# The moving weight tiles of two matmul stages, shifted by 15 distances in SBUF

## The chip, the cores and the metric

The kernel runs on one core of one Trainium2 chip. The metric is the device time in microseconds (us) of one execution; with several runs, their median. The engines are PE (TensorE, the matrix engine, whose weight loads are listed apart as PEld), DVE (VectorE), ACT (ScalarE), POOL (GpSimd) and SP (SyncE, which here only starts DMA transfers).

## The reference

One decoder layer on x of 512 tokens by 1024 channels, in float32, cut to what matters here:

```python
proj = x @ w_in                               # q, k, v, pool_in, gate logits
y_attn = moba_attention(q, k, v, rel_bias) @ w_branch_attn
y_pool = multiscale_pool(p, w_pool_group, pool_scale) @ w_branch_pool
mixed = gates[:, :, 0] * y_attn + gates[:, :, 1] * y_pool
h = layer_norm(ALPHA * x + mixed @ w_out, ln1_g, ln1_b)          # the output projection
a, u = split(h @ w_ffn_in)                                        # 1024 -> 2 x 2816
f = (gelu(causal_dwconv(a, conv_w, conv_b)) * u) @ w_ffn_out      # the FFN's output, 2816 -> 1024
out = layer_norm(ALPHA * h + f, ln2_g, ln2_b)
```

## The kernel before, in words

**Every float32 product is three matmuls.** A float32 tile is split in two tiles of type float32r: hi is a copy by ScalarE (line 75), lo is the rest by VectorE (line 76). `mm3` (lines 241 to 246) then issues hi x hi (line 242), hi x lo or lo x hi (245, 246), each a matmul with its own weight load of 128 x 128. Of each matmul one operand is *stationary* (128 columns, loaded into PE beforehand) and one is *moving* (256 or 512 columns that stream through).

**Which operand moves.** In most stages (input projection, gates, branches, FFN's input: forms p, g, br, fi, sa, sb, sc) the weights are stationary and the activations move. In two stages it is the other way round: in the output projection (`wo_mm`, form wo) and in the FFN's output (`fo_mm`, forms foa, fob, fod, foe, fo_cut) the activations (mx, sd) are stationary and the weights move, 512 columns at a time, fo_cut 256.

**Weights** come in tiles of 128 x 1024, in the order of the list `chunks`. `fetch` loads one by DMA, splits it into hi and lo, and puts these into a slot of a ring of five (`slot`, with `RING = 5`); up to three tiles are fetched ahead (`LEAD = 3`). The last three of the eight w_out tiles go to a pool of their own (`ext`). A slot is 1088 elements wide (`SLOT = D + 64`), which is 17 x 256 bytes, so all slots begin at the same place modulo 256 bytes (192 in the built program). The activations that face them begin there too, as do xT, hT and the rest. So the *distance* of a matmul, the place of its moving tile less that of its stationary tile, is 0 modulo 256 bytes, with one exception: tiles that `slot` is asked for with `near` lie `BESIDE = 2` elements, 8 bytes, further on. These are the stationary weight tiles of the first four FFN-input blocks (256-column matmuls) and of all "seven-product" tiles:

```python
o = BESIDE if near else 0
return tuple(wp.tile([P, SLOT], F32R, ...)[:, o:o + n] for q in ("hi", "lo"))
```

**Seven products.** Pairs of tiles of the input projection, gates and FFN's input, and the FFN's output as a whole, are computed by a scheme with seven products in place of eight on half-size blocks. For the pairs these are 256-column matmuls (forms sa, sb, sc: f is the FFN's input, 84 matmuls for each of 17 pairs). For the FFN's output the seven products (`PRODUCTS`: T3, B11, B21, T1, T2, B22, T4) come one after the other. Each takes six weight tiles (p, c), whose 11 half-tiles are the moving operands, against two blocks of 128 tokens: 11 x 2 x 3 = 66 matmuls. Of the last product one token block runs with 512 columns (33 matmuls, foe) and the other in two halves of 256 (66 matmuls, fo_cut). While a product runs, the next ones' operands are formed by ACT, DVE and by DMAs from POOL that add one weight block to another in place.

**Order.** The instructions are written in this order and recorded by a layer that may move them by a modelled time; no order was given by hand around the change, other than what `fetch` and `product` say.

Of the kernel before, what the change touches and what calls it, by code (L numbers as in the profile page):

```python
# [9 lines left out]
F32R = mybir.dt.float32r  # L10
# [4 lines left out]
P = 128  # L15
S = 512
D = 1024
# [15 lines left out]
RING = 5  # L33
SLOT = D + 64
BESIDE = 2
TMP = 7
PLAIN = (3, 2)
WARM = 6
RAW = 1
KH = NF // 2  # L40
# [11 lines left out]
def layer_kernel(ctx: ExitStack, tc: tile.TileContext, xT, x, w_v, w_c, rel_bias, invcnt, w_group,  # L52
# [18 lines left out]
    def split(hi, lo, src, copy=None):  # L71
        if copy:
            copy(hi, src)
        else:
            state["hi"] = nc.scalar.activation(hi, src, AF.Copy)  # L75
        state["lo"] = nc.vector.tensor_tensor(lo, src, hi.bitcast(F32), op=ALU.subtract)  # L76
        return state["lo"]
# [30 lines left out]
    WO0 = len(chunks)  # L108
    chunks += [w_out[k * P:(k + 1) * P, :] for k in range(KT)]
    FI0 = len(chunks)  # L110
# [6 lines left out]
    FO0 = len(chunks)  # L117
# [3 lines left out]

    def slot(i, n, near=False):
        o = BESIDE if near else 0
        return tuple(wp.tile([P, SLOT], F32R, tag=f"w{q}", name=f"w{q}{i}", bufs=RING)[:, o:o + n]
                     for q in ("hi", "lo"))

# [2 lines left out]
    def fetch(pool=None, early=None):  # L129
        i = state["next"]  # L130
        state["next"] = i + 1
        for q, ahead in AHEAD.items():
            while coming[q]:
                key = coming[q][0]
                n, f = key
                lead_ = EARLY.get((n, f, q), ahead)
                if not homes.get((n, q)) or at[n, f, q] > i + (lead_ if q != "A" or (n, f - 1) in pair_of else 0):
                    break
                with ExitStack() as held:
                    if (n, f, q) == ("i", 1, "X"):  # L140
                        held.enter_context(tc.issue_after(state["neg"].ins))
                    if (n, f, q) in (("i", 1, "D"), ("i", 2, "A"), ("i", 2, "X"), ("i", 2, "D")):
                        held.enter_context(tc.issue_after(state["plain"].ins))
                    if (n, f, q) == ("i", 2, "X"):
                        held.enter_context(tc.issue_after(state["sum"].ins))
                    fetch_raw(coming[q].pop(0), q)
        if isinstance(chunks[i], tuple):
            ready[i] = (fetch_fo if i >= FO0 else fetch_seven)(i, *chunks[i])
            return
        raw = wp.tile([P, D], F32, tag="wraw", name=f"wraw{i}", bufs=3)  # L150
        if pool is None:
            hi, lo = slot(i, D, FI0 <= i < FI0 + COVER)
        else:
            hi = pool.tile([P, D], F32R, name=f"whi{i}")
            lo = pool.tile([P, D], F32R, name=f"wlo{i}")
        parts = 2 if early else 1
        for c in range(parts):
            sl = slice(c * (D // parts), (c + 1) * (D // parts))
            (nc.scalar if early else nc.sync).dma_start(raw[:, sl], chunks[i][:, sl])
            split(hi[:, sl], lo[:, sl], raw[:, sl])  # L160
            if c == 0 and early:
                state["w0"] = raw[:, sl]
                early()
        ready[i] = (hi, lo)
# [10 lines left out]
    def fetch_raw(key, q):  # L175
        a, u = pair_of[key]
        r = raws[key, q] = homes[key[0], q](key[1])
        if q == "A":
            nc.sync.dma_start(r, a)
        elif q == "D":  # L180
            nc.sync.dma_start(r, u[:, S:])
        elif key in SUMMED:
            state["plain"] = nc.sync.dma_start(r[:, :S], u[:, :S])
        else:
            v = r.rearrange("p (a c) -> p a c", a=2)
            (pst, pn), (est, _) = u.ap
            state["plain"] = nc.sync.dma_start(
                v, bass.AP(tensor=u.tensor, offset=u.offset, ap=[[pst, pn], [0, 2], [est, S]]))
            state["acc"] = nc.gpsimd.dma_start(  # L189
                v, bass.AP(tensor=a.tensor, offset=a.offset, ap=[[pst, pn], [u.offset + S - a.offset, 2], [est, S]]),  # L190
                accum_op=ALU.add)

    def fetch_seven(i, key, q):
        n = S if q == "D" else D
        raw = raws[key, "A" if q == "Y" else q]
        if q == "X" and key in SUMMED:
            with tc.issue_after(state["Y"].ins):
                for c, o in ((slice(S, D), raws[key, "D"]), (slice(0, S), raws[key, "A"][:, :S])):
                    nc.vector.tensor_tensor(raw[:, c], raw[:, :S], o, op=ALU.add)
        if q == "Y":  # L200
            with ExitStack() as held:
                if key == ("f", COVER // 2):
                    held.enter_context(tc.issue_after(state["h"].ins))

                for c, o in ((slice(0, S), raws[key, "X"][:, S:]), (slice(S, D), raw[:, :S])):
                    nc.vector.tensor_tensor(raw[:, c], o, raw[:, c], op=ALU.add)
        hi, lo = slot(i, n, True)
        state[q] = split(hi, lo, raw)
        return hi, lo
# [7 lines left out]
    def fetch_fo(i, name, c):  # L217
        sl = piece(c)
        n = sl.stop - sl.start
        step = {"T3": "=B11", "B11": "+B12", "T1": "+B22", "T2": "+B21", "T4": None}  # L220
        if name in step:
            raw = tw[:, sl]
        else:
            raw = wp.tile([P, D], F32, tag="wraw", name=f"wraw{i}", bufs=3)[:, :n]
            nc.sync.dma_start(raw, half(name, sl))
        hi, lo = slot(i, n)
        split(hi, lo, raw)
        then = step.get(name)
        if then and then[0] == "+":
            nc.gpsimd.dma_start(raw, half(then[1:], sl), accum_op=ALU.add)  # L230
        elif then:
            nc.sync.dma_start(raw, half(then[1:], sl))
        return hi, lo

    def weights(i):
        while state["next"] <= min(i + LEAD, state["limit"]):
            fetch()
        return ready[i]
# [102 lines left out]
    for kt in range(KT):  # L341
        xk = xr[kt // 4][:, kt % 4, :]
        if kt == 0:
            load_x(kt, xk, slice(0, 256), nc.vector.tensor_copy)
            fetch(early=lambda: load_x(kt, xk, slice(256, 512), nc.vector.tensor_copy))
        else:
            load_x(kt, xk)
            if kt % 2 == 0:
                fetch()
# [102 lines left out]
    def pool_sum(j, b, sign=1.0, eng=None):  # L452
        eng = eng or nc.gpsimd
        w = POOL_WINDOWS[j]
        pt = pb.tile([P, PAD + S], F32, tag="tmp", name=f"pt{j}", bufs=TMP)
        nc.gpsimd.memset(pt[:, :PAD], 0.0)
        state["pt"] = nc.scalar.activation(pt[:, PAD:], b, AF.Copy, scale=sign)
        cur, sh = pt, 1
        while sh < w:
            nxt = pb.tile([P, PAD + S], F32, tag="tmp", name=f"pw{j}_{sh}", bufs=TMP)  # L460
            o = 2 * sh - 1
# [251 lines left out]
    def gate_done(f, ba, u):  # L713
        if f < KT - 1:
            for br, v, scale in ((0, ba, 1.0), (1, u, -1.0)):
                nc.scalar.activation(v, v, AF.Sigmoid, scale=scale)
                nc.vector.tensor_tensor(branch[f, br], branch[f, br], v, op=ALU.mult)
            merged(f, branch[f, 0], branch[f, 1])
        else:
            for br, v, scale in ((0, ba, 1.0), (1, u, -1.0)):  # L720
                gslot[8 * br + f] = unused.pop(0)
                nc.scalar.activation(gslot[8 * br + f], v, AF.Sigmoid, scale=scale)
# [6 lines left out]
    for f in range(GSEVEN, KT):  # L729
        if f == KT - 1:  # L730
# [3 lines left out]
              lambda ba, u, f=f: gate_done(f, ba, u), first_half if f == KT - 1 else None)  # L734
# [427 lines left out]
```

## Time and profile before

| what | us |
|---|---|
| timed runs, median of 3 | 627.9 |
| timed runs, lowest and highest | 627.87, 630.2 |
| profiled execution, span from first to last instruction | 625.9 |
| PE busy in the span | 616.0 (98%) |
| DVE, ACT, POOL busy | 505.2, 353.8, 119.0 |
| output projection, from its first matmul to its end | 245.19 to 290.49 |
| the FFN's output, from its first matmul to its last one's end | 512.19 to 617.28 |

How to read it: the profiled execution is one run of its own; its span lies 2.0 us under the median of the timed runs. "Busy" of PE counts matmuls from start to a modelled end, and they overlap; the time that one matmul takes of the stream is therefore read from start to start in a timeline, or as a stretch's length divided by its number of matmuls. A group by form gives the mean from start to modelled end, in ns, which differs from the step to the next start by a constant, so that differences between forms carry over.

### The profile page before, as it was taken

To read this page: it belongs to the slowest core of one execution; us is meant where nothing else is said; L and a number is where in the kernel's file an instruction comes from. 1 tells how busy PE (TensorE), PEld (TensorE's weight loads), DVE (VectorE), ACT (ScalarE), POOL (GpSimd) and SP (SyncE) were. 2 spreads that over 40 slices of the span, in tenths; PEclk is the share of its full clock that TensorE was granted. 3 is DMA by queue.
4 is the path that set the end of the run, shared out by engine and by line. 5 is a ranking of instruction groups with operands and counts; after the bars stand their busy time and mean duration, and the time that the engine had idled before them with its cause. 6 is when DMAs were issued, how large, how long until landed. Compare 5 with 4: busy or idle time off the path is not lost.

```text
span 625.9 us, 10417 instructions
## 1 busy us (share of the span) xinstructions
PE 616.0 (98%) x3988; PEld 552.9 (88%) x3988; DVE 505.2 (81%) x780; ACT 353.8 (57%) x536; POOL 119.0 (19%) x131
## 2 busy tenths in 40 slices
PE   8999999999999999999999999999999999999994
PEld 6899998777788998889999999999999888888884
DVE  6978787776494788399998988898988869798886
ACT  6646777655644567125566565566656346555442
POOL 0133134323132101110110101101100302123302
PEclk9999999999999999999999999999999999999998
DMA  9566647422548515816668687687745996899805
GB/s 321 163 193 187 177 121 223 134 78 78 169 111 211 149 60 177 293 43 225 146 167 208 184 201 185 176 201 201 187 97 161 325 254 127 221 192 207 195 1 134
DMA packets 40545, 107.70 MB, mean 172 GB/s; under 512 B 4384, under 2 KB 4648, under 8 KB 40240
## 3 DMA queue, kind: packets, MB, share of 16 engines
q1 hardware_dynamic: 27264, 71.90, 34.8%
q0 software_dynamic: 12656, 34.10, 28.0%
q10 hardware_dynamic: 576, 1.05, 0.5%
q8 instruction: 31, 0.51, 0.4%
q14 instruction: 18, 0.15, 0.1%
HBM read 102.82 MB, written 3.17 MB: 169 GB/s over the span
## 4 chain that ended last, share of the span: by engine, by line
PE 98%; DVE 1%; DMA 1%; DVEq 0%; issue 0%
PE saf L242 5%; PE saf L245 5%; PE saf L246 5%; PE v L420 3%; PE fi L242 3%; PE fi L245 3%; PE fi L246 3%; PE sbf L242 3%; PE sbf L246 3%; PE sbf L245 2%; PE br L242 2%; PE g L242 2%; PE g L246 2%; PE g L245 2%; PE wo L242 2%; PE br L246 2%
## 5 line engine op out<-in xcount | busy, mean ns | idle before, releaser
L75 ACT ACTIVATE whi<-wraw 128x1024 fp32r<-128x1024 f32 (+1 forms) x53 | 53.8, 1023 | 39.6 <-DMA wraw<-in_w_fo 8.1
L76 DVE TENSOR_TENSOR wlo<-wraw,whi 128x1024 fp32r<-128x1024 f32 (+1 forms) x53 | 65.1, 1235 | 12.7 <-ACT whi L75 12.5
L76 DVE TENSOR_TENSOR wlo<-araw,whi 128x1024 fp32r<-128x1024 f32 x52 | 63.3, 1225 | 9.4 <-ACT whi L75 9.1
L75 ACT ACTIVATE whi<-araw 128x1024 fp32r<-128x1024 f32 x52 | 54.4, 1058 | 20.2 <-PE saf L245 5.6
L189 POOL DMA_DIRECT2D xraw<-in_w_fi x15 | 18.0, 1203 | 135.9 <-DMA xraw<-in_w_fi 69.2
L75 ACT ACTIVATE whi<-tw 128x1024 fp32r<-128x1024 f32 (+1 forms) x30 | 29.5, 983 | 25.4 <-DMA tw<-in_w_fo 10.7
L76 DVE TENSOR_TENSOR wlo<-tw,whi 128x1024 fp32r<-128x1024 f32 (+1 forms) x30 | 33.5, 1129 | 9.0 <-ACT whi L75 9.0
L242 PE MATMUL sbf<-T_hi,whi 128*128 128x256 f32 x136 | 37.9, 279 | 0.0
L242 PE MATMUL saf<-hT_hi,whi 128*128 128x256 f32 x136 | 37.9, 279 | 0.0
L242 PE MATMUL saf<-nT_hi,whi 128*128 128x256 f32 x136 | 37.8, 278 | 0.0
L245 PE MATMUL saf<-hT_lo,whi 128*128 128x256 f32 x136 | 37.8, 278 | 0.0
L246 PE MATMUL saf<-nT_hi,wlo 128*128 128x256 f32 x136 | 37.8, 278 | 0.0
L246 PE MATMUL sbf<-T_hi,wlo 128*128 128x256 f32 x136 | 37.7, 278 | 0.0
L245 PE MATMUL sbf<-T_lo,whi 128*128 128x256 f32 x136 | 37.7, 277 | 0.0
L245 PE MATMUL saf<-nT_lo,whi 128*128 128x256 f32 x136 | 37.7, 277 | 0.0
L246 PE MATMUL saf<-hT_hi,wlo 128*128 128x256 f32 x136 | 37.6, 277 | 0.0
L245 PE MATMUL fi<-hT_lo,whi 128*128 128x256 f32 (+1 forms) x112 | 36.2, 326 | 0.0
L246 PE MATMUL fi<-hT_hi,wlo 128*128 128x256 f32 (+1 forms) x112 | 36.2, 325 | 0.0
L242 PE MATMUL fi<-hT_hi,whi 128*128 128x256 f32 (+1 forms) x112 | 36.1, 327 | 0.0
L560 POOL TENSOR_SCALAR pp<-pp,rs 128x128 f32<-128x128 f32 (+3 forms) x32 | 25.2, 803 | 36.7 <-DVE rs L557 26.6
L230 POOL DMA_DIRECT2D tw<-in_w_fo x18 | 15.6, 896 | 61.4 <-DVE wlo L76 61.4
L555 ACT ACTIVATE pp<-pp,nm 128x128 f32<-128x128 f32 (+3 forms) x32 | 17.6, 551 | 14.8 <-DVE nm L552 14.8
(346 smaller groups left out, 2171.8 us busy)
## 6 DMA issues: line engine op xcount, KB each, us to landing
tw<-in_w_fo POOLq DMA_DIRECT2D x20, 512.0 KB, 8.1
araw<-in_w_fi SPq DMA_DIRECT2D x17, 512.0 KB, 3.9
xraw<-in_w_fi SPq DMA_DIRECT2D x15, 512.0 KB, 4.3
xraw<-in_w_fi POOLq DMA_DIRECT2D x15, 512.0 KB, 6.2
wraw<-in_w_c SPq DMA_DIRECT2D x10, 512.0 KB, 4.4
wraw<-in_w_fi SPq DMA_DIRECT2D x10, 512.0 KB, 3.7
wraw<-in_w_fo SPq DMA_DIRECT2D x10, 512.0 KB, 5.1
tw<-in_w_fo SPq DMA_DIRECT2D x10, 512.0 KB, 7.5
```

The costliest lines, as they stand in the source:

```text
L75: state["hi"] = nc.scalar.activation(hi, src, AF.Copy)
L76: state["lo"] = nc.vector.tensor_tensor(lo, src, hi.bitcast(F32), op=ALU.subtract)
L189: state["acc"] = nc.gpsimd.dma_start(v, bass.AP(tensor=a.tensor, offset=a.offset, ap=[[pst, pn], [u.offset + S - a.offset, 2], [est, S]]), ...
L230: nc.gpsimd.dma_start(raw, half(then[1:], sl), accum_op=ALU.add)
L242: ins = nc.tensor.matmul(out_, wh, ah, start=start, stop=False, **kw)
L245: nc.tensor.matmul(out_, wh, al, start=False, stop=False, **kw)
L246: nc.tensor.matmul(out_, wl, ah, start=False, stop=stop, **kw)
L420: ins = nc.tensor.matmul(bs[j], xs_[j][a], (wh, wl)[b], start=kt == 0 and n == 0, stop=False)
L555: exps[h] = nc.scalar.activation(pp[:, offs[i]:offs[i] + n], pp[:, offs[i]:offs[i] + n], AF.Exp, bias=nm[:, i:i + 1], accum_out=rs[:, i:i ...
L560: nc.gpsimd.tensor_scalar(pp[:, offs[i]:offs[i] + n], pp[:, offs[i]:offs[i] + n], rs[:, i:i + 1], 1.0, op0=ALU.mult, op1=ALU.mult)
```

## The change

`slot` gives the moving weight tiles of the two stages a start that depends on the tile (w_out) or on the product (w_ffn_out). The table's numbers are bytes. For w_out each of the 8 tiles has its own distance; for the FFN's output each of the seven products has one for its six tiles: T3 8 (foe), B11 16 (foa), B21 24 (fob), T1 40 (fod), T2 72 (foa), B22 128 (fod), T4 200 (foe and fo_cut). The stationary operands stay where they are.

```diff
 BESIDE = 2
+APART = {"wo": (8, 16, 24, 32, 48, 56, 64, 96), "fo": (8, 16, 24, 40, 72, 128, 200)}
 ...
     def slot(i, n, near=False):
         o = BESIDE if near else 0
+        if WO0 <= i < FI0:
+            o = APART["wo"][i - WO0] // 4
+        elif i >= FO0:
+            o = APART["fo"][(i - FO0) // ((KH + 1) // 2)] // 4
 ...
         else:
-            hi = pool.tile([P, D], F32R, name=f"whi{i}")
-            lo = pool.tile([P, D], F32R, name=f"wlo{i}")
+            o = APART["wo"][i - WO0] // 4
+            hi, lo = (pool.tile([P, D + 32], F32R, name=f"w{q}{i}")[:, o:o + D] for q in ("hi", "lo"))
```

The three tiles in the pool `ext` become 128 bytes wider. Packed one behind the other they then begin, modulo 256, at the former place (hi) and 128 bytes beyond it (lo); with their offsets the distances are 56, 64, 96 for hi and 184, 192, 224 for lo. All other addresses are as before, and the instructions of every engine stand in the same order. One ScalarE instruction (the first split of T4_hi, which takes the place of such a tile) waits in addition for a signal of ScalarE itself that lies 28 signals back.

## Rows read from the trace of the kernel before

**Rows 1.** The page: busy time, share of the span, instructions; granted clock; chain.

```profile
PE 616.0 (98%) x3988; PEld 552.9 (88%) x3988; DVE 505.2 (81%) x780; ACT 353.8 (57%) x536; POOL 119.0 (19%) x131
...
PE 98%; DVE 1%; DMA 1%; DVEq 0%; issue 0%
```

**Rows 2.** Busy time by stretch: output projection, second and fifth product, last product.

```profile
core 0: us, PE busy (x) PEld busy (x) DVE busy (x) ACT busy (x) POOL busy (x), PEclk, DMA share, GB/s
245.19:277.40 32.21, 32.21 (x144) 26.67 (x143) 22.03 (x43) 8.89 (x13) 7.21 (x7) 1.00 0.51 182
277.40:290.49 13.09, 13.09 (x68) 11.06 (x66) 12.27 (x23) 8.71 (x14) 0.00 (x0) 1.00 0.35 100
...
527.15:542.11 14.96, 14.96 (x67) 12.39 (x66) 11.80 (x13) 7.49 (x8) 3.47 (x4) 1.00 1.05 231
...
572.03:586.99 14.96, 14.96 (x67) 12.39 (x66) 11.14 (x12) 8.41 (x9) 6.71 (x5) 1.00 1.02 257
...
601.95:617.28 15.33, 15.33 (x100) 13.97 (x98) 13.26 (x33) 6.91 (x10) 1.90 (x3) 1.00 0.30 45
```

**Rows 3.** Timeline of PE, third product: start us, us to modelled end.

```profile
550.04 0.39 PE L246 MATMUL fob<-whi,sd_lo 128*128 128x512 f32 x1
...
550.73 0.39 PE L246 MATMUL fob<-whi,sd_lo 128*128 128x512 f32 x1
```

**Rows 4.** Timeline of PE, last product's 256-column matmuls, first and eleventh of a sequence.

```profile
614.88 0.28 PE L242 MATMUL fo_cut<-whi,sd_hi 128*128 128x256 f32 x1
...
616.08 0.28 PE L245 MATMUL fo_cut<-wlo,sd_hi 128*128 128x256 f32 x1
```

**Rows 5.** Timeline, saf, first and seventh of a sequence; busy time, 320 to 470 us.

```profile
399.74 0.28 PE L246 MATMUL saf<-nT_hi,wlo 128*128 128x256 f32 x1
...
400.43 0.28 PE L245 MATMUL saf<-hT_lo,whi 128*128 128x256 f32 x1
...
320.00:470.00 150.00, 150.00 (x1301) 1.00 0.73 185
```

**Rows 6.** Groups of PE by form: busy us, mean ns of one, idle before.

```profile
L242 PE MATMUL saf<-hT_hi,whi 128*128 128x256 f32 x136 | 37.9, 279 | 0.0
L246 PE MATMUL saf<-hT_hi,wlo 128*128 128x256 f32 x136 | 37.6, 277 | 0.0
L242 PE MATMUL fob<-whi,sd_hi 128*128 128x512 f32 x22 | 8.6, 389 | 0.0
L245 PE MATMUL fo_cut<-wlo,sd_hi 128*128 128x256 f32 x22 | 6.2, 283 | 0.0
```

**Rows 7.** Groups of PEld (weight loads) by form, same columns.

```profile
L242 PEld LDWEIGHTS saf<-hT_hi,whi 128*128 128x128 f32 x136 | 25.5, 188 | 0.0
L242 PEld LDWEIGHTS fob<-whi,sd_hi 128*128 128x128 f32 x22 | 4.1, 188 | 0.9
L242 PEld LDWEIGHTS fo_cut<-whi,sd_hi 128*128 128x128 f32 x22 | 4.2, 191 | 0.2
```

**Rows 8.** Groups of PE, 200.5 to 200.8 us (br before sag), 290.2 to 290.4 (wo before fi).

```profile
L246 PE MATMUL br<-oT_hi,wlo 128*128 128x512 f32 x1 | 0.4, 391 | 0.0
L242 PE MATMUL br<-oT_hi,whi 128*128 128x512 f32 x1 | 0.4, 389 | 0.0
...
L246 PE MATMUL wo<-whi,mx_lo 128*128 128x512 f32 x1 | 0.4, 391 | 0.0
```

**Rows 9.** Groups of ACT and DVE by form: the splits at offset 8 (araw) and 0 (tw).

```profile
L75 ACT ACTIVATE whi<-araw 128x1024 fp32r<-128x1024 f32 x52 | 54.4, 1058 | 20.2 <-PE saf L245 5.6 <-PE scf L245 3.5 <-PE sai L245 2.6
L75 ACT ACTIVATE whi<-tw 128x1024 fp32r<-128x1024 f32 x25 | 26.3, 1054 | 20.4 <-DMA tw<-in_w_fo 10.7 <-PE fod L246 5.9 <-PE fob L246 1.9
L76 DVE TENSOR_TENSOR wlo<-araw,whi 128x1024 fp32r<-128x1024 f32 x52 | 63.3, 1225 | 9.4 <-ACT whi L75 9.1
L76 DVE TENSOR_TENSOR wlo<-tw,whi 128x1024 fp32r<-128x1024 f32 x25 | 30.3, 1220 | 9.0 <-ACT whi L75 9.0
```

**Rows 10.** Waits, 512 to 626 us: us in total, times, longest us.

```profile
ACT whi L75 <- PE fod L246: 7.0, 6, 1.9
```

## Prediction

> **What bounds the kernel now.** I read the page first [rows 1]: TensorE (PE) is busy 98% of the span, and the chain that ended last runs over PE for 98% of its length. So whatever makes a matmul of this program longer or shorter goes into the time, and whatever another engine does goes in only if PE comes to wait for it. Then the stages that the change touches, in the busy times by stretch [rows 2]: the output projection (two stretches, 45.3 us with 16 transposes between them), and the FFN's output, products one to six of 14.96 us each (six rows alike in this, two shown), then the last product. [...] A product is 66 matmuls of 512 columns (11 k x 2 token blocks x 3), so one takes 14.96 / 66 = 226.7 ns from start to start. The timeline shows the same: 550.04 to 550.73 is three matmuls in 0.69 us [rows 3].
>
> Next the question that the change asks: does a matmul take longer or shorter by where its moving tile lies, against the stationary tile that is loaded beside it? The trace of before holds two distances. The 512-column matmuls and the last product's 256-column ones (fo_cut) have distance 0 mod 256. The many 256-column matmuls of the seven-product tiles (saf, sbf) have their stationary tiles 8 bytes off, through BESIDE. Between these the timeline differs: fo_cut starts every 120 ns (614.88 to 616.08, ten steps) [rows 4], saf every 115.5 ns (399.74 to 400.43, six steps, 115; and 150 us with 1301 matmuls that touch the stretch, 115.3 to 115.5) [rows 5]. The groups by form agree: 283 ns from start to modelled end against 277 to 279, with the weight load (PEld) 191 ns against 188 [rows 6, 7]. So 8 bytes go with 4.5 ns less per matmul at 256 columns.
>
> [...]
>
> **The change part by part.** It reorders nothing and adds no instruction; only start addresses move. By its tiles: the output projection has 8 tiles x 2 token halves x 4 token blocks x 3 = 192 matmuls of 512 columns; the FFN's output 6 x 66 + 33 = 429 of 512 columns and 66 of 256. That is 621 long and 66 short.
>
> *The 66 short ones (fo_cut, 200 bytes).* They stand where 256-column matmuls are slow, and leave distance 0. If 200 does what 8 does in saf: 66 x 4.5 = 0.3 us less. If the distance does not matter, 0. I take the 0.3.
>
> *The 621 long ones.* No row has them steadily at another distance. Bounds from both sides. Gain: the 4.5 ns of the short ones, 621 x 4.5 = 2.8 us. Further: 256 more columns cost 389 - 283 = 106 ns [rows 6], so 512 bare columns would be 212 ns and 14.7 ns of the 226.7 is surplus; all of it gone is 9.1 us. Loss: where a 512-column matmul is followed by a weight load from a tile 8 bytes off, it takes 391 ns instead of 389 [rows 8]; there are 14 such changes of shape, and none of those that do not wait for something is shorter than its neighbours. 621 x 2 = 1.2 us. If the loss were as large as the gain at 256, 2.8 us. Which is nearest? In fo_cut the slow cadence comes with a slow weight load (191 against 188). In the long matmuls at distance 0 the weight load takes 188, as in saf [rows 7]: nothing holds it up, and at 188 ns it is over before the next matmul starts (226.7), which it is not at 256 columns (120). What a distance relieves at 256 columns is thus not seen at 512, and the only direct rows (391) point the other way by little. I take 0 for the long ones, with both ends kept.
>
> *Writers of the moved tiles.* ScalarE and VectorE now write hi and lo at other offsets. Tiles 8 bytes off already stand in the trace: whi<-araw (off by 8) 1058 ns against whi<-tw (off by 0) 1054, wlo<-araw 1225 against wlo<-tw 1220 [rows 9]. That is 5 ns on engines that are ahead of PE: in the FFN's output their waits are for PE to free the ring's buffers (ScalarE's splits 7.0 us on fod in six waits) [rows 10]. Cost 0. If the cover were gone, some 50 splits x 10 ns is 0.5 us. *The added wait* in front of one split of T4_hi is for a ScalarE signal 28 signals back on the same engine: 0. *The widened tiles* of the last three w_out tiles put their lo parts 128 bytes further on than their hi parts; this is only another distance.
>
> Sum: the profiled execution's span is 625.9 us; less 0.3 is 625.6. The median of the timed runs is 627.9, 2.0 more than the span, so I forecast 627.6 us. That is the same within what a measurement of this kernel tells from no change (0.5%, 3.1 us).
>
> **The rivals.**
> (1) *The long matmuls gain as the short ones did.* For: nothing in the code treats them differently, and both have distance 0 before. Against: the 188 ns weight load. If only distances that are odd multiples of 8 relieve (8, 24, 56 and 184; 8, 24, 40, 72, 200): 72 + 264 + 33 long and 66 short = 435 matmuls x 4.5 = 2.0 us, 625.9. If all do: 687 x 4.5 = 3.1 us, 624.8.
> (2) *The whole surplus goes* at some distances that no row here has. For: 14.7 ns stand above the bare columns. Against: 8 bytes took only 4.5 of the 14 that fo_cut has above 106 (120 - 106). At all distances it would be 9.1 + 66 x 14 = 0.9, so 10.0 us and 617.9; at half of them 622.9. Then the ring would be late next: DMA engines are busy for 1.02 to 1.05 of the stretch in the second and fifth product [rows 2].
> (3) *Slower: moving reads from a shifted start collide more.* Place: each of the 621 long matmuls, which now are in step with their stationary tile and would not be. For: 391 against 389 [rows 8]. Against: at 256 columns the cadence settled to 115 where it was out of step. Price: 2 ns each is 1.2 us, 629.1; 4.5 ns each is 2.8 us, 630.7. It decides from 3.1 us / 621 = 5 ns per matmul on, which is about the whole difference between fo_cut and saf. [...]
> (4) *It does nothing at all*: the 115.5 comes from the stationary tile's own place and not from the distance, or from the shape of the work around it. For: in the trace only stationary tiles were shifted, no moving one. 627.9.
>
> **How the numbers follow.** Forecast 0.35 and rival (4) 0.12, which a measurement cannot part: 0.47. Rival (1): 0.23, of which a part lies beyond 0.5%. Rival (2): 0.08. Rival (3): 0.22, of which 0.07 beyond 5 ns per matmul. Faster by over 0.5% (under 624.8): all of (2) and 0.05 of (1), 0.13. Slower (over 631.0): 0.07. Within: 0.80. Range: from 624.8, the far end of (1), to 630.4, just under the 4.5 ns end of (3); left out are (2), and the ends of (1) and (3). The likeliest case alone is 627.2 to 628.2. The runs of before themselves reach from 627.87 to 630.2.
>
> **What would show it.** In the profile after, each product of the FFN's output has its own distance and so its own stretch. Right: all six stay at 14.96 us, foa, fob, fod and foe at 389 ns, only fo_cut goes from 283 to about 278 and its weight load from 191 to 188. Rival (1): the products at 8, 24, 40, 72 fall to 66 x 222.2 = 14.66 us, those at 16 and 128 stay. Rival (2): a product under 14.5 us, or ScalarE no longer waiting for PE. Rival (3): a product above 15.1 us, or forms at 391 or more. Rival (4): fo_cut stays at 283. The forecast fails if the products part by more than 0.3 us, in either direction, or if PE gets idle time between 245 and 617 us.

## The result, and the profile after

The changed kernel takes 632.39 us (median of 4 runs, 631.88 to 632.68), the kernel before 629.04 in the runs beside it (627.87 to 630.2). The ratio is 1.006, interval 1.0041 to 1.008: 0.6% slower, where 627.6 and "no change" was forecast with 630.4 as the upper end. Part of the way to 632.39 lies in the kernel before: two of its four runs beside the new ones took 630.2, and the forecast had started from 627.9.

PE is as full as before, and the chain still runs over it. First the page of the kernel after (busy time, share of the span, instructions), which answers to [rows 1]:

```profile
PE 620.5 (98%) x3988; PEld 553.8 (88%) x3988; DVE 506.2 (80%) x780; ACT 354.5 (56%) x536; POOL 118.3 (19%) x131
```

The span grew from 625.9 to 630.2 us, PE's busy time by 4.5, with the same 3988 matmuls. Next the busy time by stretch, as in [rows 2]: the output projection as a whole, the six products with distances 8, 16, 24, 40, 72, 128, and the last product (200).

```profile
core 0: us, PE busy (x) PEld busy (x) DVE busy (x) ACT busy (x) POOL busy (x), PEclk, DMA share, GB/s
245.49:291.85 46.36, 46.36 (x210) 37.85 (x208) 34.37 (x65) 18.16 (x27) 7.19 (x7) 1.00 0.45 159
513.56:529.04 15.48, 15.48 (x68) 12.50 (x66) 13.72 (x15) 10.91 (x13) 2.23 (x3) 1.00 0.54 137
529.04:544.33 15.29, 15.29 (x68) 12.42 (x67) 11.57 (x13) 8.46 (x10) 2.96 (x4) 1.00 0.99 226
544.33:559.73 15.40, 15.40 (x67) 12.41 (x66) 12.32 (x13) 8.60 (x11) 2.21 (x3) 1.00 0.69 169
559.73:575.13 15.40, 15.40 (x68) 12.44 (x66) 13.79 (x18) 8.58 (x10) 5.72 (x8) 1.00 1.03 172
575.13:590.66 15.53, 15.53 (x67) 12.47 (x66) 11.72 (x12) 8.56 (x10) 5.94 (x5) 1.00 0.99 248
590.66:606.02 15.36, 15.36 (x68) 12.46 (x67) 12.08 (x18) 6.55 (x7) 0.00 (x0) 1.00 0.26 60
606.02:621.63 15.61, 15.61 (x100) 14.14 (x98) 13.25 (x33) 6.87 (x10) 2.03 (x3) 1.00 0.32 46
```

Each product was 14.96. Together they took 92.46 - 89.76 = 2.70 us more, the output projection 46.36 - 45.30 = 1.06, the last product 0.16 (15.61 against 15.45: before, it begins at 601.95, its last matmul starts at 617.28, which the table before calls the end, and that one's step ends at 617.40). That is 3.92 of the span's 4.3; another 0.30 comes from ahead of the first moved tile (the output projection begins at 245.49, not 245.19). That is within what this part varies by: in two kernels below that change nothing ahead of the output projection (only sd_lo moved; sd0 and sd1 moved by 8 and 64) it begins at 245.13 and 246.19. PE is busy in the whole of each stretch and the granted clock is 1.00, so nothing was waited for and nothing was throttled: the matmuls themselves follow each other more slowly. The timeline of the third product (start us, us to modelled end) answers to [rows 3]:

```profile
549.70 0.40 PE L251 MATMUL fob<-whi,sd_lo 128*128 128x512 f32 x1
549.93 0.40 PE L247 MATMUL fob<-whi,sd_hi 128*128 128x512 f32 x1
550.16 0.40 PE L250 MATMUL fob<-wlo,sd_hi 128*128 128x512 f32 x1
550.40 0.40 PE L251 MATMUL fob<-whi,sd_lo 128*128 128x512 f32 x1
```

Three steps are 0.70 us, 233 ns each, where they were 226.7 to 0.01. The groups by form, first of matmuls, then of weight loads (busy us, mean ns of one, idle before), answer to [rows 6, 7]:

```profile
L247 PE MATMUL saf<-hT_hi,whi 128*128 128x256 f32 x136 | 37.9, 279 | 0.0
...
L251 PE MATMUL fob<-whi,sd_lo 128*128 128x512 f32 x22 | 8.7, 397 | 0.0
L250 PE MATMUL fob<-wlo,sd_hi 128*128 128x512 f32 x22 | 8.7, 396 | 0.0
L247 PE MATMUL fob<-whi,sd_hi 128*128 128x512 f32 x22 | 8.7, 396 | 0.0
...
L250 PE MATMUL fo_cut<-wlo,sd_hi 128*128 128x256 f32 x22 | 6.2, 283 | 0.0
```

```profile
L247 PEld LDWEIGHTS fo_cut<-whi,sd_hi 128*128 128x128 f32 x22 | 4.2, 189 | 0.2
...
L247 PEld LDWEIGHTS fob<-whi,sd_hi 128*128 128x128 f32 x22 | 4.1, 188 | 1.0
```

The 512-column matmul went from 389 to 396 or 397, while its weight load stayed at 188. The form that was not touched (saf) stayed where it was. By the start times in the trace, the mean step of a 512-column matmul is now, by distance of the FFN's output: 8 bytes 234.5 ns, 16 231.7, 24 233.4, 40 233.3, 72 235.4, 128 232.5, 200 233.0; in the output projection 232.4 over all its distances. No distance kept a mean of 226.7. (3.92 - 0.05) / 621 = 6.2 ns more per long matmul, where the 0.05 is what fo_cut lost (119.3 to 120.1 ns).

### The profile page after: what moved, and what is told of

Same layout as the page of the kernel before. It is cut to its first block, busy times and chain, and to the rows that moved or that the text cites. A ratio compares the mean times of both kernels' runs of the same rounds, so it can differ in the third digit from the quotient of the medians.

```text
span 630.2 us, 10418 instructions
## 1 busy us (share of the span) xinstructions
PE 620.5 (98%) x3988; PEld 553.8 (88%) x3988; DVE 506.2 (80%) x780; ACT 354.5 (56%) x536; POOL 118.3 (19%) x131
## 4 chain that ended last, share of the span: by engine, by line
PE 98%; DVE 1%; DVEq 0%; issue 0%
PE saf L247 5%; PE saf L251 5%; PE saf L250 5%; PE v L425 3%; PE fi L247 3%; PE fi L251 3%; PE fi L250 3%; PE sbf L247 3%; PE sbf L251 2%; PE sbf L250 2%; PE wo L247 2%; PE wo L250 2%; PE wo L251 2%; PE br L247 2%; PE g L250 2%; PE g L247 2%
## 5 line engine op out<-in xcount | busy, mean ns | idle before, releaser
L235 POOL DMA_DIRECT2D tw<-in_w_fo x18 | 15.6, 896 | 63.1 <-DVE wlo L77 63.1
L560 ACT ACTIVATE pp<-pp,nm 128x128 f32<-128x128 f32 (+3 forms) x32 | 17.6, 552 | 15.3 <-DVE nm L557 15.2
```

The costliest lines, as they stand in the source:

```text
L560: exps[h] = nc.scalar.activation(pp[:, offs[i]:offs[i] + n], pp[:, offs[i]:offs[i] + n], AF.Exp, bias=nm[:, i:i + 1], accum_out=rs[:, i:i ...
```

## The experiments

All are the kernel before, or the changed kernel with another table `APART`. In five of them the stationary tiles of the FFN's output are moved as well, by

```diff
+    def shifted(pool, name, o):
+        t = pool.tile([P, KH * 256 + 64], F32R, name=name)
+        return t[:, o // 4:o // 4 + KH * 256].rearrange("p (a c) -> p a c", a=KH)
```

in place of `pool.tile([P, KH, 256], ...)` for sd0 (products one, three, five, seven) and sd1 (two, four, six). "Distance" is moving tile less stationary tile, modulo 256 bytes, as before. Steps in ns without a row are means of the differences between start times in the trace. Rows of busy times with PE alone hold: the stretch, its length, PE busy and its matmuls, granted clock, DMA share, GB/s. Where no ratio stands, a kernel ran once.

### Is it the distance? Both moved by 8 bytes

```diff
+APART = {"wo": (0, 0, 0, 0, 0, 0, 0, 0), "fo": (8, 8, 8, 8, 8, 8, 8)}
+                sd = [tuple(shifted(sq, f"sd0_{q}", o) for q, o in (("hi", 8), ("lo", 8)))]
+    sd.append(tuple(shifted(fp, f"sd1_{q}", o) for q, o in (("hi", 8), ("lo", 8))))
```

> All seven products of the FFN's output have their moving weight tiles at 8 bytes, and their stationary tiles sd are moved by 8 bytes too, so that the distance is 0 again; the output projection is as before. Theory D (the distance between the moving tile and the stationary tile counts): each of products one to six is back at 14.96 us, 389 ns from start to modelled end, 226.7 ns per matmul, and the time is that of the kernel before (629.0 us, within 0.3). Theory A (the moving tile's own place modulo 256 bytes counts): the products stay at about 15.4 us each, and the time is 2.8 us above before, near 632.

Measured: 630.17 us against 628.15, ratio 1.0033 (1.0022 to 1.0044). The busy times of the first, second and sixth product:

```profile
512.25:527.52 15.27, 15.27 (x68) 1.00 0.53 138
527.52:542.78 15.26, 15.26 (x67) 1.00 1.01 228
588.60:603.87 15.27, 15.27 (x67) 1.00 0.30 64
```

15.27 / 66 = 231.4 ns: better than 234.5 with the moving tile alone at 8, but not the 226.7 of before. Neither theory holds as it was put. Distance 0 is not enough. The rows also speak against one more rival, that other traffic slows the matmuls: at DMA shares of 0.53, 1.01 and 0.30 the step is the same.

### Which of three matmuls pays? Only sd_lo moved by 8

```diff
+                sd = [tuple(shifted(sq, f"sd0_{q}", o) for q, o in (("hi", 0), ("lo", 8)))]
+    sd.append(tuple(shifted(fp, f"sd1_{q}", o) for q, o in (("hi", 0), ("lo", 8))))
```

> The moving tiles are where they were before; only the lo parts of the stationary tiles sd lie 8 bytes further on. Of each three matmuls the third uses sd_lo (line 246 of before), and its weights are loaded while the second streams (line 245). Theory D, if what counts is the weight load that runs beside the stream: the second of each three takes some 6 ns more (steps of 233 against 227), the third none; a product is 66 x 2 = about 0.13 us longer. If the tile's own stationary partner counts: the third takes more and the second none. Theory A (the moving tile's own place): nothing changes, 226.7 everywhere.

Measured: a product takes 15.25 us, 0.29 more than before and not 0.13. The groups of the third product by form:

```profile
L242 PE MATMUL fob<-whi,sd_hi 128*128 128x512 f32 x22 | 8.7, 395 | 0.0
L246 PE MATMUL fob<-whi,sd_lo 128*128 128x512 f32 x22 | 8.6, 393 | 0.0
L245 PE MATMUL fob<-wlo,sd_hi 128*128 128x512 f32 x22 | 8.6, 392 | 0.0
```

All three are longer than 389, and the longest is the one whose moving tile, own weights and next weights all lie where they lay before (L242). All three expectations miss; the second of each three (L245), which was to pay, is the shortest. Two things follow. The moving tiles did not move here, so it is not the moving tile's place alone. And a matmul's step depends on what ran before it: an operand out of place delays its neighbours too, so the cost can't be booked to one pair of tiles.

### Other distances, by the moving tile and by the stationary tile

```diff
+APART = {"wo": (4, 252, 248, 244, 240, 160, 112, 80), "fo": (4, 252, 248, 240, 224, 192, 12)}
```

> Other distances of the moving tiles: products at 4, 252 (4 before), 248, 240, 224, 192, 12 bytes; w_out tiles at 4, 252, 248, 244, 240, 160, 112, 80 (hi and lo alike). If only distance 0 gives the short step, every product takes 15.2 to 15.6 us, and the FFN's output and the output projection together some 3.9 us more than before. If the sign counts as at 256 columns, where 248 gave 115.5 against 120 ns, then the product at 248 falls below 14.96 us (14.66 at 4.5 ns less per matmul). If a distance of 4 bytes is too small to matter, the products at 4 and 252 stay at 14.96.

The busy times of products one to six, distances 4, 252, 248, 240, 224, 192:

```profile
514.34:530.02 15.68, 15.68 (x67) 1.00 0.56 141
530.02:545.06 15.04, 15.04 (x67) 1.00 0.98 224
545.06:560.34 15.28, 15.28 (x68) 1.00 0.67 169
560.34:575.74 15.40, 15.40 (x68) 1.00 1.02 175
575.74:591.14 15.40, 15.40 (x68) 1.00 1.00 246
591.14:606.52 15.38, 15.38 (x67) 1.00 0.28 61
```

The run took 632.06 us against 628.15, the 3.9 more that was expected, but the products spread wider than 15.2 to 15.6. None falls below 14.96. 252 (4 bytes back) comes nearest with a mean of 227.9 ns, and this is a mix: 46 of its 66 steps are 226 or 227 ns, the others 229 to 232. 4 bytes forward is the worst, 237.6 ns. The sign does not carry over from 256 columns: 248, the good one there, costs 231.4 here. The output projection's tiles agree: 236 ns at 4, some 230 at 252, 112 and 80, the others 232 to 237. Here too the means hide two kinds of steps. In one stretch, at the tiles with distances 112 and 80, thirteen steps in a row (first and last start shown) are short with no tile at distance 0:

```profile
263.92 0.39 PE L247 MATMUL wo<-whi,mx_hi 128*128 128x512 f32 x1
...
266.87 0.39 PE L250 MATMUL wo<-wlo,mx_hi 128*128 128x512 f32 x1
```

That is 226.6 ns each by the start times in the trace; when the tile at 112 is used again, for the other token blocks, its mean step is 232.

The next kernel moves the stationary tiles instead, sd0 by 8 and sd1 by 64 bytes:

```diff
+                sd = [tuple(shifted(sq, f"sd0_{q}", o) for q, o in (("hi", 8), ("lo", 8)))]
+    sd.append(tuple(shifted(fp, f"sd1_{q}", o) for q, o in (("hi", 64), ("lo", 64))))
```

> The moving tiles stay; only the stationary tiles sd are moved, by 8 bytes in products one, three, five, seven and by 64 in two, four, six: distances 248 and 192, made from the other side than before. Moved by the moving tile, 248 gave 231.4 ns and 192 gave 233.2. Theory D (distance alone): the same 231.4 and 233.2. If the own place of each tile counts too, other values, but above 226.7; if only the moving tile's place counts, 226.7. fo_cut (256 columns, 248) should go from 120 to about 115.6 as saf.

The busy times of products one (248) and two (192), then fo_cut's forms (248):

```profile
513.20:528.43 15.23, 15.23 (x68) 1.00 0.51 135
528.43:543.82 15.39, 15.39 (x67) 1.00 1.03 233
```

```profile
L246 PE MATMUL fo_cut<-whi,sd_lo 128*128 128x256 f32 x22 | 6.1, 279 | 0.0
L242 PE MATMUL fo_cut<-whi,sd_hi 128*128 128x256 f32 x22 | 6.1, 278 | 0.0
```

230.7 and 233.3 ns: within 0.7 ns of 231.4 and 233.2 for the same distances made with the moving tile. So distance does count, from whichever side it is made. And fo_cut goes from 282 or 283 to 278 or 279: at 256 columns 8 bytes do what they do in saf.

### What else must hold? Both moved by 64 and 16, by 128 and 32

In two kernels moving and stationary tiles move alike, by 64 or 128 bytes in products one, three, five, seven, and by 16 or 32 in two, four, six.

```diff
+APART = {"wo": (0, 0, 0, 0, 0, 0, 0, 0), "fo": (64, 16, 64, 16, 64, 16, 64)}
+APART = {"wo": (0, 0, 0, 0, 0, 0, 0, 0), "fo": (128, 32, 128, 32, 128, 32, 128)}
```

> Moving and stationary tiles of the FFN's output are moved by the same amount, so that the distance is 0: by 64 bytes in products one, three, five and seven, by 16 in two, four and six. With both at 8 the step was 231.5 ns, not 226.7. [...] Theory C (only the former place modulo 256 bytes gives the short step): none returns, all at 15.2 or more.

The busy times of products one to four:

```profile
513.17:528.17 15.00, 15.00 (x67) 1.00 0.57 151
528.17:543.56 15.39, 15.39 (x67) 1.00 0.99 225
543.56:558.57 15.01, 15.01 (x67) 1.00 0.69 170
558.57:573.96 15.39, 15.39 (x67) 1.00 1.01 172
```

64 returns (227.3 ns), 16 does not (233.2).

> As with 64 and 16, moving and stationary tiles moved alike, by 128 bytes in products one, three, five, seven and by 32 in two, four, six. Theory B (for the short step at 512 columns the distance is 0 and both begin at a multiple of 64 bytes): 128 gives 227 to 228 ns and 15.0 us per product, 32 gives 231 to 234 and 15.2 to 15.4. If a multiple of 32 is enough, both give 227.

The busy times of products one to four of this kernel:

```profile
516.97:531.94 14.97, 14.97 (x67) 1.00 0.52 140
531.94:546.95 15.01, 15.01 (x68) 1.00 1.03 229
546.95:561.96 15.01, 15.01 (x67) 1.00 0.72 176
561.96:576.97 15.01, 15.01 (x68) 1.00 1.02 176
```

32 and 128 both return (227 to 228 ns), which also shows that the wider sd tiles alone cost nothing. (This kernel's single time of 632.7 us says nothing on the FFN's output: PE was idle for 2.7 us between 300 and 350 us, ahead of it.) So in these runs the 512-column matmuls have the short step throughout where two things hold: moving and stationary tile begin at the same place modulo 256 bytes, and that place is a multiple of 32 (tried: the former place and 32, 64 and 128 bytes beyond it against 8 and 16 beyond it). The stretch at 112 and 80 and most steps at 252 show that the short step can also occur without them; there it did not last. Theory B's 64 was too strict, and both at 8 failed by the second condition.

### The 4.5 ns at 256 columns: undone, and scanned

```diff
-BESIDE = 2
+BESIDE = 0
```

> BESIDE = 0: the 256-column matmuls are at distance 0 as well, which undoes the 8 bytes that the prediction took its 4.5 ns from. If these are worth 4.5 ns at each of the 2350 short matmuls, the steps are 120 and the time is 10.6 us above before, about 639. If 120 is only one of several steady values at distance 0, some stretches stay at 116 to 118 and it is less.

Measured: 638.58 us against 628.17, 10.4 more. Of the 2184 steps in the forms of the pairs (sa, sb, sc of input projection, gates and FFN's input), 2076 are 120 ns. The group of saf by form, against 279 in [rows 6]:

```profile
L242 PE MATMUL saf<-hT_hi,whi 128*128 128x256 f32 x136 | 38.6, 284 | 0.0
```

The prediction's reading of [rows 4, 5] was right to a few per cent. A scan then gave each of the 17 pairs its own offset of the stationary tiles (the lines of one scan; the other differs in its numbers):

```diff
+BESIDES = (0, 4, 8, 12, 16, 24, 32, 48, 64, 96, 128, 160, 192, 224, 240, 248, 252)
+        if key and key[0] == "f":
+            o = BESIDES[key[1] - SEVEN[0]] // 4
```

> The stationary tiles of the FFN input's 17 pairs, 84 matmuls of 256 columns each, lie at 17 offsets (0, 4, 8, 12, 16, 24, 32, 48, 64, 96, 128, 160, 192, 224, 240, 248, 252 bytes) in place of 8, so that the distances are 0, 252, 248 down to 4. Theory D: the pair at offset 0 takes 120 ns per matmul and the one at 8 takes 115.5; the others lie between 115 and 126, as fo_cut does at distance 200 (120.1 mean over its three forms), and the whole is up to 6 us slower. If any distance other than 0 relieves 256-column matmuls, all but the first pair are at 115.5 and the time is that of before.

> As the first scan of the 256-column pairs, at 17 other offsets of the stationary tiles: 36, 40, 44, 52, 56, 60, 64, 68, 72, 76, 80, 88, 104, 112, 120, 144, 176 bytes. If the gain at 64 lies in its being a multiple of 64 with the load half or a quarter of 256 bytes ahead, only 64 is at 113.7 and its neighbours are at 116 to 122. If it is a smooth valley, the neighbours at 60 and 68 are between. If 64 was luck, it is not at 113.7 again, since another pair has it now.

| offset, bytes | mean step, ns |
|---|---|
| 0, 4, 8, 12 | 119.2, 118.4, 115.6, 116.7 |
| 16, 24, 32, 48 | 118.4, 121.0, 122.5, 118.2 |
| 36, 40, 44, 52, 56 | 119.6, 119.3, 118.1, 115.0, 118.0 |
| 60, 64, 68, 72, 76 | 119.9, 113.7 and 115.5, 118.4, 118.3, 115.5 |
| 80, 88, 96, 104 | 118.8, 114.4, 118.8, 119.7 |
| 112 to 252 (11 values) | 117.6 to 119.9 |

The two scans took 632.61 and 631.15 us. The valley is not smooth, and 64, 88 and 52 seemed to beat 8. Set for all tiles, 64 and 88 do not:

```diff
-BESIDE = 2
+BESIDE = 16     # the other kernel: 22
```

> The kernel before with BESIDE = 16 elements (64 bytes) in place of 2: all stationary tiles of 256-column matmuls lie 64 bytes off, the moving weight tiles of the two stages where they were. In the scan of offsets the pair at 64 bytes took 113.7 ns per matmul against 115.6 at 8. If that holds for all of them, some 2350 x 1.9 = 4.5 us less than before, about 624 (0.7% faster). If 113.7 was the luck of one pair, no change, 628 to 629.

> BESIDE = 22 elements (88 bytes) in place of 2, nothing else changed. In the second scan the pair at 88 bytes took 114.4 ns per matmul, 8 bytes take 115.6. If that holds, 2350 x 1.2 = 2.8 us less than before, about 625.5. But at 64 bytes one pair had 113.7 in the first scan, another 115.5 in the second, and all together 117.8: the step at one offset has more than one steady value. If 88 behaves so, it is 117 to 119 ns and 3 to 8 us slower.

Measured: at 64 bytes 632.78 us against 628.48, ratio 1.0057 (1.0036 to 1.0077); at 88 bytes 629.8 against 628.17, ratio 1.0022 (1.0013 to 1.0031). Neither gain came; 64 bytes are slower than the "no change" of their expectation, 88 less slow than the 3 to 8 us of theirs. Steps are 117.8 and 116.3, and at 88 bytes they part by stage: 116.6 in the FFN's pairs (1428 matmuls) but 113.5 in the gates' pairs (336, where the kernel before has 115.6), as the groups by form show:

```profile
L246 PE MATMUL saf<-nT_hi,wlo 128*128 128x256 f32 x136 | 37.9, 279 | 0.0
L246 PE MATMUL sag<-gnT_hi,wlo 128*128 128x256 f32 x32 | 8.8, 276 | 0.0
```

Here is the timeline at offset 64, first of the scan and then of the kernel with 64 everywhere (nine and eight steps from first to last row):

```profile
399.08 0.28 PE L245 MATMUL saf<-nT_hi,whi 128*128 128x256 f32 x1
...
400.10 0.28 PE L245 MATMUL sbf<-T_hi,whi 128*128 128x256 f32 x1
```

```profile
400.29 0.28 PE L246 MATMUL saf<-nT_hi,wlo 128*128 128x256 f32 x1
...
401.23 0.28 PE L245 MATMUL saf<-nT_lo,whi 128*128 128x256 f32 x1
```

113.3 against 117.5 ns for the same matmuls of the same pair at the same distance: the stream has more than one steady step at one offset. The two kernels differ in the offsets of the pairs around this one, so what runs beside or before it is the likely cause; no run separates that further. A scan that gives each short stretch its own offset therefore does not tell the step that the offset has over the whole stream. No kernel here beats the kernel before.

## Why the prediction was wrong, point by point

**What bounds the kernel** held: PE has no wait in the stages after either, and the 3.9 us of longer steps came back in the span, which grew by 4.3.

**The 621 long ones** is the step that failed: "I take 0 for the long ones". They lost 6.2 ns each, 3.9 us in all, and the experiments show by what: a start of the moving tile that differs, modulo 256 bytes, from that of the stationary tile. The two reasons given for 0 were weak in the same way. The weight load of 188 ns was taken to mean that nothing stands between load and stream at 512 columns; after the change it is still 188 with the matmul at 397, so this duration says nothing about the step. And the only direct row [rows 8] did show a loss, 391 against 389, but of single matmuls at changes of shape, from which 2 ns was taken as the size. In a steady stream it is three times that.

**The bounds** were cut too narrow by symmetry. The end on the losing side was "as large as the gain at 256", 4.5 ns and 630.7 us; nothing in the trace tied the loss at 512 columns to the gain at 256. Of the seven distances of the FFN's output, all lost some 5 ns or more.

**Rival (3)** was the right one in place and sign: each long matmul, from the moment that it is out of step with its stationary tile. It was said to decide from 5 ns on; 6.2 came. Its picture of colliding reads was only argued, and no run shows what collides. At distances 16 and 128 the step is 231.7 and 232.5 ns against 226.7, and with both operands moved by 16 bytes it is 233.2, so multiples of 16 bytes are not enough for the short step.

**Rival (4)**, no effect at all, is out at 512 columns by the moving tile (231.7 to 235.4 ns) and by the stationary tile as well: with the moving tile untouched, moving only the stationary tile took the step from 226.7 to 230.7 and 233.3.

**Rivals (1) and (2)** are out: no distance gave a product a mean step under 226.7. Of the split by odd multiples of 8 little shows: here they take 233.0 to 235.4 ns against 231.7 and 232.5 at 16 and 128, so they lose more and not less, and in the other scan 248 takes 231.4 against 233.2 to 233.3 at 240, 224 and 192.

**The 66 short ones** should have given 0.3 us, and lost 0.05. The premise (8 bytes are worth 4.5 ns at 256 columns) was right, as BESIDE = 0 and fo_cut at 248 show; but "200 does what 8 does" was not: its step was 120.1.

**Writers, added wait, order** cost nothing, as forecast: the split to whi<-tw takes 1055 ns (1054 before), that to wlo<-tw 1221 (1220).

**What stays open**: why the same place modulo 256 and a multiple of 32 bytes make the step short, why the step carries over from one matmul to the next, why some stretches at other distances run at the short step, and whether another order of the three matmuls would change it.

## What to carry to other kernels

Where PE is the bound, the start addresses of the two matmul operands are part of the time: 6 ns on 227, or 3%, for each long matmul here. As far as these runs go, keep the moving and the stationary tile of 512-column matmuls at the same place modulo 256 bytes and that at a multiple of 32, and try 8 bytes between them only where the moving tile has 256 columns (115.6 ns against 120.0 here). When no row shows a case, bound it by what the operation could lose, not by what its neighbour gained, and try an offset over the whole stream, not over a short stretch of it.

## What was not expected of the hardware

- Distance 0, with both tiles at a multiple of 32 bytes, is the best at 512 columns (226.7 to 227.6 ns; means of 227.9 to 237.6 at other distances), and distance 0 is one of the worst at 256 (120.0; 8 bytes 115.6).
- 4 bytes matter: at 512 columns 237.6 ns at distance 4, 227.9 at 252.
- One offset can have two steady steps (113.3 and 117.5 ns at 64 bytes, 256 columns), and at 512 columns too a distance can show the short step in one stretch and not in another (226.6 and 232 ns at 112 bytes).
- The weight load's duration (188 to 192 ns) does not follow the step.
